# Spreading the gates of a product-key expert layer: bf16 one-hot rows for eight tokens, three gate parts summed in PSUM, splits on VectorE

## The chip, the cores and the metric

One core of one Trainium2 chip runs the whole program in one launch. The metric is the device time of that launch in microseconds, lower is better; the traces give the span from the first to the last instruction of one profiled execution. A core has TensorE (PE, its weight loads shown as PEld), VectorE (DVE), ScalarE (ACT), GpSimd (POOL) and SyncE (SP, which issues the loads here).

## The reference, cut to what matters

256 tokens of width 1024 pass a first block (a delta-net mixer and an expert layer with product keys, PEER) and then a second block of two layers (a token mixer and a routed expert layer each). The change lies in PEER, whose 16384 experts are the pairs of 128 first and 128 second keys:

```python
q = (xt @ w_q).reshape(T, 8, 2, 128)                    # 8 heads, two halves
s = einsum('thpd,hpkd->thpk', q, sub_keys)              # scores against 128 keys each
s1, i1 = top_k(s[:, :, 0], 16); s2, i2 = top_k(s[:, :, 1], 16)
cand_s = s1[..., :, None] + s2[..., None, :]            # 256 candidates
cand_i = i1[..., :, None] * 128 + i2[..., None, :]
top_s, pos = top_k(cand_s, 16); idx = take(cand_i, pos) # 16 experts per head
gate = softmax(top_s)
hid = einsum('td,thkd->thk', xb, u_tab[ib])
coef = gelu(hid) * gb
y = einsum('thk,thkd->td', coef, v_tab[ib])
```

## The kernel before, in words

PEER is computed densely over the experts. `utile(i, tb, eng)` (L917) makes the hidden values of 128 experts (one first key, 128 second keys) for all 256 tokens: `esplit` (L902) loads 128 x 1024 weights (512 KB) into one of three raw places, `split_w` (L39) makes their two parts, the high one on ScalarE (L44) and the low one on the engine that `eng` names (L46), each with three buffers, and `hidden` (L908) multiplies in three passes (L52 to L54), 24 matmuls of 256 columns. ScalarE applies Gelu for the tokens whose gates aren't there yet (L922); for the first `tb` tokens, whose gates are, it goes to `eh` (L925) and VectorE multiplies it into the gates (L926). There are 128 such tiles. The array G[second key, first key, token] holds hidden values, gates and at last their products.

`peer_route` (L928) runs in two stages. In the first, `query(h)` (L945) makes a head's two queries from weights split on GpSimd and `score` their scores; `choose(h)` (L969) takes, on VectorE, the 16 largest of each half (`top16`, L1077), of the 256 sums, and by comparing and reducing (L986 to L994) the two key numbers of each chosen pair, for both halves of the tokens in one go. Behind each head come four hidden tiles, their low parts made on GpSimd, and the query of the head after the next. Softmax gives the gates. Key numbers and gates are then transposed, so that the 128 pairs (head, rank) of a token lie on the partitions (L1024, L1025).

In the second stage G's gates are made by matmul. For four tokens at a time, `onehots` (L1036) compares the key numbers with 0 to 127: L1041 gives the rows of the first key, L1042 those of the second, in f32; L1043 multiplies the first by the high part of the gates, and four ScalarE instructions L1045 by the low part. `spread` (L1048) multiplies the rows of each token, 256 columns (two gate parts side by side, L1052). `gates` (L1054) copies the low sums to SBUF on ScalarE (L1057) and adds the high ones on VectorE, for the experts whose hidden values aren't there (L1059), and for those that are (L1060) with a product by them (L1061). G is written with the tokens innermost, so each token's values are 1 KB apart. Each turn makes one hidden tile besides, with `tb = t0 + 4`.

`peer_experts` (L1086) makes the remaining hidden tiles and multiplies the 128 tiles of values: `vparts` (L1093) splits a value tile on VectorE, and the coefficients into `ech` and `ecl` (L1097, L1098); `vmul` runs 12 matmuls of 512 columns.

The order on each engine is set by the tile framework's scheduler, which takes ready instructions in program order by a model of costs; an engine then works through its queue in that order and waits where an operand isn't there.

Of the kernel before, what the change touches and what calls it, by code (L numbers as in the profile page):

```python
# [33 lines left out]
class Ker:  # L34
# [3 lines left out]
    # ---------------------------------------------------------------- helpers  # L38
    def split_w(self, raw, pool, bufs, tag, eng="gpsimd"):  # L39
        """the two exact parts of raw, in float32r tiles of its shape"""  # L40
        nc = self.nc
        hi = pool.tile(list(raw.shape), F32R, name=tag + "h", bufs=bufs)
        lo = pool.tile(list(raw.shape), F32R, name=tag + "l", bufs=bufs)
        nc.scalar.activation(hi[:], raw, AF.Copy)  # L44
        e = nc.gpsimd if eng == "gpsimd" else nc.vector
        e.tensor_tensor(lo[:], raw, hi[:].bitcast(F32), ALU.subtract)  # L46
        return hi, lo

    def mm3(self, out, L, R, first, last):
        """out += L^T R for operands split in two parts (three passes of float32r)."""  # L50
        mm = self.nc.tensor.matmul
        mm(out, L[0], R[0], start=first, stop=False)  # L52
        mm(out, L[0], R[1], start=False, stop=False)  # L53
        mm(out, L[1], R[0], start=False, stop=last)  # L54

    def consts(self, st):
# [14 lines left out]
        # factors of the rows' norms, sums of squares  # L71
# [3 lines left out]
    def silu_cols(self, cp):  # L75
        """stationary operands of the modulation products"""
# [7 lines left out]
        # stationary operands of the modulation products: 32 columns for each k chunk  # L84
# [9 lines left out]
    # ------------------------------------------------------------ modulations  # L94
    def ada_third(self, key, w, bias, t, wp, wbufs, pp, pt, wk):
        """columns t*2048.. of silu(c) @ w + bias: kept as columns, and as rows in DRAM."""
# [27 lines left out]
        for s in range(ns):  # L124
            # (g, c) order: column 512 g + 128 c
# [3 lines left out]
    def col(self, key, s, chunk):  # L129
        """[128, 8]: the chunk-th 1024 values of the modulation, one column for each k."""  # L130
# [3 lines left out]
    def gate_bcast(self, key, chunk, dst, o=0, w=1024):  # L134
        """dst [128, w] = the chunk-th 1024 values of the modulation from the o-th on, on every partition."""
# [4 lines left out]
    def rstd(self, pool, src, n, mul, add, name):  # L140
        """(src * mul + add) ** -0.5 for src [128, n]"""
# [6 lines left out]
    def rows(self, make, order=((0, 0), (0, 1), (1, 0), (1, 1))):  # L148
        """make(i, j) makes half j of the rows of token tile i of x and returns a place for the squares;
        1/32 of the factors of the rows' norm"""  # L150
# [10 lines left out]
    def norm_T(self, pool, pt, g_cols, sh_cols, dst):  # L161
        """dst(k, ..) <- transpose of x times the row factors, with the column scale and shift"""
# [12 lines left out]
    def mod_parts(self, hh, hl, pool):  # L175
        """dst of norm_T: the two parts of the modulated values, the work shared by three engines"""
# [13 lines left out]
    # ------------------------------------------------------------- delta net  # L190
    def slot(self, n=1):
        """lets the work in the background advance"""
# [10 lines left out]
    def until(self, key):  # L203
        """places are free only after the work of the key"""
# [3 lines left out]
    def delta(self):  # L208
# [12 lines left out]
        # a large negative number where a strictly lower-triangular matrix has zeros  # L221
# [12 lines left out]
        # the projections that come with the norm, and their sums' places  # L234
# [33 lines left out]
    def delta_in(self, cx):  # L268
        """the normed tokens, modulated, a chunk of 128 channels at a time; the first projections follow"""
# [45 lines left out]
        def products(k):  # L315
            """of the vectors' silu and the weights, in four groups of rows"""
# [8 lines left out]
        def columns(k):  # L325
            """shift and scale of the channels, and the two parts of the modulated values"""
# [31 lines left out]
    def delta_gates(self):  # L358
        """beta and the log decays, tokens on partitions: [128, block, (direction, head)]"""
# [28 lines left out]
        # exp of the running sums: eG up to and with a token, eR over those after it, gl over the block  # L388
# [8 lines left out]
        # scalars of the state products: -beta eG (forward), -eG (backward)  # L397
# [4 lines left out]
    def prep(self):  # L402
        """loads and splits the next projection's weights, in two halves"""
# [28 lines left out]
    def conv_silu2(self, ps, ci, ntok):  # L432
        """twice silu of the convolved channels [128, ntok]"""
# [28 lines left out]
    def transposes(self, srcs, pool=None):  # L462
        """one bank with the transposes of up to four blocks"""
# [8 lines left out]
    def l2(self, tp, nb, extra, dst):  # L472
        """dst <- tp / 2 normed over the last axis, times extra ** -0.5"""
# [8 lines left out]
    def gmul(self, out, in0, in1):  # L482
        """out = in0 * in1 on GpSimd"""
        self.nc.gpsimd.tensor_tensor(out, in0, in1, ALU.mult)

    # keys: convolved, normed, and the matrices A of the chunks' systems (I + A) x = b
# [53 lines left out]
    # values and queries  # L540
# [30 lines left out]
    # twice silu of the gate with the norm's weight, tokens on partitions  # L571
# [17 lines left out]
    # in the background  # L589
# [23 lines left out]
    def y_task(self):  # L613
        """the normed, gated output's transposes in two parts"""
# [95 lines left out]
    def delta_out(self):  # L710
        """the output projection, half of its columns and of its rows at a time"""
# [3 lines left out]
        # the output weights take the residual's gate  # L715
# [28 lines left out]
    def add_rows(self, acc, order=((0, 0), (0, 1), (1, 0), (1, 1)), scale=None, gate=None):  # L744
        """x <- x (times the scale of its rows) + acc (times the gate), and the factors of its norm"""
# [12 lines left out]
    def softplus(self, pool, out, x, shape):  # L758
        """max(x, 0) + log1p(exp(-|x|)), the logarithm as 2 atanh(e / (2 + e)) in its series"""
# [18 lines left out]
    def blk_inverse(self, M):  # L778
        """M <- transposes (forward) or the inverses themselves (backward) of I + A, for the 32 strictly
        lower-triangular A in M"""  # L780
        nc, bp, wk, px = self.nc, self.bp, self.wk, self.px
        L = wk.tile([128, 32, 32], F32, name="Lt")   # (r, problem) on partitions: [j][i] = A[i, j]
        T = wk.tile([128, 32, 32], F32, name="Tt")   # [i][c]
        Xc = wk.tile([128, 32, 32], F32, name="Xc", tag="Lt")  # (r, i) on partitions: [problem][c]
# [61 lines left out]
        def s4(q):  # L846
            if q % 2 == 1:  # backward: the inverse itself
# [11 lines left out]
    # ------------------------------------------------------------------ PEER  # L859
    def peer(self):  # L860
        """dense over the experts: hidden values of 128 experts at a time for all tokens, times the
        gates of the chosen ones (zero elsewhere), times the experts' rows"""
# [8 lines left out]
        # the first weights come before the norm  # L871
        self.first = [self.esplit(a["peer_wq"][p], "v") for p in range(2)]
        self.xd = self.dram.tile([128, 2, D], F32, name="xd")
        with ExitStack() as s1:
# [6 lines left out]
            # the residual waits in DRAM; its place takes weights  # L881
# [11 lines left out]
    def rawt(self):  # L893
        """a place for 128 x 1024 raw weights"""
# [7 lines left out]
    def esplit(self, src, eng):  # L902
        """128 x 1024 weights from DRAM in their two parts"""
# [4 lines left out]
    def hidden(self, *Ws):  # L908
        """[128 columns of W, 256 tokens] of the products with the normed tokens, for each W"""
# [7 lines left out]
    def utile(self, i, tb, eng):  # L917
        """hidden values of experts 128 i ..: times the gates for the first tb tokens, whose gates are there"""
# [9 lines left out]
    def peer_route(self, G):  # L928
        """G <- gates, times the hidden values of the first experts, whose number is returned"""
# [4 lines left out]
        idT = [kp.tile([128, 256], F32, name=f"idT{p}") for p in range(2)]  # L934
        gT = kp.tile([128, 256], F32, name="gaT")
# [9 lines left out]
        def query(h):  # L945
# [8 lines left out]
            for p in range(2):  # L954
                ps = P[p] or self.hidden(self.esplit(a["peer_wq"][2 * h + p], "gpsimd"))[0]
# [6 lines left out]
        def score():  # L962
            """of the last query, behind the products that follow it"""
# [5 lines left out]
        def choose(h):  # L969
            sc = wk.tile([128, 2, 2, 128], F32, name="sc", bufs=1)  # L970
            nc.scalar.activation(sc[:], scores[h][:], AF.Copy)
            for i in range(2):
# [3 lines left out]
                for p in range(2):  # L976
                    self.top16(sc[:, i, p, :], v[:, p, :], ix[:, p, :], wk, 128)
                nc.vector.tensor_copy(fx[:], ix[:])
# [4 lines left out]
                self.top16(cand[:].rearrange("p a b -> p (a b)"), top[:, i, h, :], pos[:], wk, 256)  # L983
                ab = wk.tile([128, 2, 16], U32, name="ab")
# [4 lines left out]
                for p in range(2):  # L989
# [4 lines left out]
                    nc.vector.tensor_reduce(sel[p][:, i, h, :], oh[:], mybir.AxisListType.X, ALU.add)  # L994
        ge = []

        def softmax():
            """of the chosen scores"""
# [11 lines left out]
        for h in range(NH):  # L1010
            choose(h)
            if h == NH - 1:
                softmax()
            for _ in range(4):
                self.utile(nu, 0, "gpsimd")
                nu += 1
                score()
            if h + 2 < NH:
                query(h + 2)
        # slots (head, rank) on partitions  # L1020
        for i in range(2):
            tp = pt.tile([128, 4, 128], F32, name="tp")
            for n, (src, dstT) in enumerate(((sel[0][:, i], idT[0]), (sel[1][:, i], idT[1]), (ge[i][:], gT))):
                nc.tensor.transpose(tp[:, n, :], src.rearrange("p h s -> p (h s)"), self.ident)  # L1024
                nc.vector.tensor_copy(dstT[:, i * 128:(i + 1) * 128], tp[:, n, :])  # L1025
        s1.close()
        wk = st.enter_context(tc.tile_pool(reuse_waits="tile", name="p_o", bufs=2))
        ps_g = st.enter_context(tc.tile_pool(reuse_waits="tile", name="p_sg", bufs=2, space=PSUM))
        iota = self.sm("iota").unsqueeze(1).to_broadcast([128, 4, 128])
        # the gates in two exact parts, whose sums come side by side  # L1030
        gh, gl = [kp.tile([128, 256], F32R, name=f"ga{p}") for p in "hl"]
        nc.scalar.activation(gh[:], gT[:], AF.Copy)
        nc.vector.tensor_sub(gl[:], gT[:], gh[:].bitcast(F32))
# [1052 lines left out]
```

## Time and profile before

| | |
|---|---|
| Time, median of 3 runs | 2524.61 us (2518.95 to 2528.83) |
| Profiled execution, span from first to last instruction | 2511.5 us |
| Its time outside the span | not recorded by itself; the median lies 13.1 us above the span |
| Choosing the keys, with 32 hidden tiles | 572 to 763 us of the span |
| Spreading the gates, with 67 hidden tiles | 763 to 1131 us |
| The other hidden tiles, with values | 1131 to 1294.5 us |
| Values alone | 1294.5 to 1566 us |

The stages were cut at the first instructions of the lines that begin them: the copy of the first head's scores (L971), the first one-hot product (L1041), the first coefficients (L1097); and at the end of the last hidden tile's product (L926). How to read it: a share of busy time over the span averages over these stages, so the stages are to be read one by one; and an engine that waits with an instruction already begun counts as busy.

### The profile page before, as it was taken

The numbers are of one execution on the slowest core, as the hardware profiler recorded it, in microseconds if no ns is written. First come the engines' busy times: TensorE is split into PE (matmuls) and PEld (weight loads), VectorE is DVE, ScalarE is ACT, GpSimd is POOL, SyncE is SP. The second block draws the span as 40 slices with busy tenths as digits, with TensorE's granted clock in tenths as the row PEclk, the third lists the DMA queues.
The fourth block names the chain that finished last, engine by engine and source line by source line (L and its number), as shares of the span: only waits on it lengthen the run. The fifth ranks groups of instructions, "written<-read, shape, count | busy, mean of one in ns | idle before, by whom it ended". The sixth has DMA issues, their size and how long they took to land. (4 is left out here: it accounts for less than half of the span.)

```text
span 2511.5 us, 36197 instructions
## 1 busy us (share of the span) xinstructions
PE 2266.3 (90%) x13220; PEld 1619.1 (64%) x13220; DVE 1596.0 (64%) x3069; ACT 950.9 (38%) x2012; POOL 664.9 (26%) x496
## 2 busy tenths in 40 slices
PE   7999999989877777669999999898999989989997
PEld 5445666659877766668988888776444357744432
DVE  4786572458999999994457677877232259733323
ACT  3433434434335555554443333434221133432111
POOL 2443212346644444544420000323000014200000
PEclk9999999989988888989999999999999989989999
DMA  6566564654433232226655555664999636579981
GB/s 255 164 210 191 163 191 154 202 187 157 137 104 109 93 97 92 89 93 195 205 189 190 188 189 181 218 214 150 344 409 386 217 130 216 174 276 407 396 301 60
DMA packets 152607, 497.54 MB, mean 198 GB/s; under 512 B 16960, under 2 KB 18496, under 8 KB 150880
## 3 DMA queue, kind: packets, MB, share of 16 engines
q1 hardware_dynamic: 152416, 495.09, 57.5%
q8 instruction: 108, 1.77, 0.3%
q14 instruction: 83, 0.68, 0.1%
HBM read 492.86 MB, written 2.16 MB: 197 GB/s over the span
## 5 line engine op out<-in xcount | busy, mean ns | idle before, releaser
L52 PE MATMUL hps<-ph,esh 128*128 128x256 f32 x1152 | 349.8, 304 | 25.7 <-ACT G L922 21.5
L54 PE MATMUL hps<-ph,esl 128*128 128x256 f32 x1152 | 347.7, 302 | 8.6 <-POOL esl L46 8.5
L53 PE MATMUL hps<-pl,esh 128*128 128x256 f32 x1152 | 347.1, 301 | 1.0 <-POOL pl L187 1.0
L46 POOL TENSOR_TENSOR esl<-x,esh 128x1024 fp32r<-128x1024 f32 x95 | 244.1, 2572 | 256.1 <-ACT esh L44 237.1
L1898 PE MATMUL pg<-wgu,xe 128*64 128x512 f32 x1024 | 276.3, 601 | 0.0
L52 PEld LDWEIGHTS hps<-ph,esh 128*128 128x128 f32 x1152 | 243.9, 212 | 29.1 <-ACT G L922 23.0
L44 ACT ACTIVATE esh<-x 128x1024 fp32r<-128x1024 f32 x170 | 179.4, 1055 | 207.0 <-PE y L54 120.6
L54 PEld LDWEIGHTS hps<-ph,esl 128*128 128x128 f32 x1152 | 242.4, 210 | 10.8 <-POOL esl L46 10.8
L53 PEld LDWEIGHTS hps<-pl,esh 128*128 128x128 f32 x1152 | 243.1, 211 | 2.3 <-POOL pl L187 1.2
L52 PE MATMUL y<-esh,ech 128*128 128x512 f32 x512 | 201.7, 394 | 1.3 <-ACT esh L44 1.3
L54 PE MATMUL y<-esh,ecl 128*128 128x512 f32 x512 | 202.0, 394 | 0.0
L53 PE MATMUL y<-esl,ech 128*128 128x512 f32 x512 | 201.9, 394 | 0.0
L1898 PEld LDWEIGHTS pg<-wgu,xe 128*64 128x64 f32 x1024 | 79.0, 137 | 131.8 <-issue 123.9
L1041 DVE TENSOR_TENSOR om<-small,idT 128x512 f32<-128x512 f32 x64 | 155.2, 2425 | 1.7 <-ACT o L1045 1.7
L46 POOL TENSOR_TENSOR esl<-raw,esh 128x1024 fp32r<-128x1024 f32 x47 | 120.4, 2561 | 107.8 <-ACT esh L44 100.9
L106 PE MATMUL adaps<-adaw,cst 128*32 128x512 f32 x512 | 139.7, 608 | 9.7 <-DMA adaw<-in_ada_w_dram 5.9
L46 DVE TENSOR_TENSOR esl<-x,esh 128x1024 fp32r<-128x1024 f32 x75 | 91.9, 1226 | 86.9 <-ACT esh L44 86.9
L1052 PE MATMUL gp<-o,o 128*128 128x256 f32 x256 | 50.2, 323 | 98.5 <-ACT esh L44 77.6
L44 ACT ACTIVATE esh<-raw 128x1024 fp32r<-128x1024 f32 x92 | 97.1, 1056 | 99.9 <-PE y L54 68.9
L46 DVE TENSOR_TENSOR wrsl<-wr,wrsh 128x512 fp32r<-128x512 f32 x135 | 104.5, 788 | 34.9 <-ACT wrsh L44 33.9
L1930 PE MATMUL pw<-wdn,hTs 128*64 128x512 f32 x512 | 124.1, 597 | 0.0
L1045 ACT ACTIVATE o<-om,gal 128x128 fp32r<-128x128 f32 x256 | 81.8, 390 | 108.3 <-DVE om L1041 105.7
(610 smaller groups left out, 4925.2 us busy)
## 6 DMA issues: line engine op xcount, KB each, us to landing
wgu<-in_w_gu_dram SPq DMA_DIRECT2D x256, 512.0 KB, 10.2
wdn<-in_w_d_dram SPq DMA_DIRECT2D x128, 512.0 KB, 7.4
adaw<-in_w_ada_dram SPq DMA_DIRECT2D x96, 512.0 KB, 4.3
x<-in_peer_u_dram SPq DMA_DIRECT2D x81, 512.0 KB, 3.7
x<-in_peer_v_dram SPq DMA_DIRECT2D x75, 512.0 KB, 4.3
raw<-in_peer_u_dram SPq DMA_DIRECT2D x47, 512.0 KB, 3.9
raw<-in_peer_v_dram SPq DMA_DIRECT2D x43, 512.0 KB, 4.3
dw<-in_dn_w_dram SPq DMA_DIRECT2D x64, 256.0 KB, 4.5
```

Of the source, the lines that this page charges most:

```text
L44: nc.scalar.activation(hi[:], raw, AF.Copy)
L46: e.tensor_tensor(lo[:], raw, hi[:].bitcast(F32), ALU.subtract)
L52: mm(out, L[0], R[0], start=first, stop=False)
L53: mm(out, L[0], R[1], start=False, stop=False)
L54: mm(out, L[1], R[0], start=False, stop=last)
L106: nc.tensor.matmul(ps[g * 32:(g + 1) * 32, :], self.cst[:, which, k, :], wt[:, v * 512:(v + 1) * 512], start=k == 0, stop=k == KC - 1)
L1041: nc.vector.tensor_tensor(m[:], iota, b(idT[0]), ALU.is_equal)
L1045: nc.scalar.activation(o1[:, t, 1, :], m[:, t, :], AF.Copy, scale=gl[:, t0 + t:t0 + t + 1].bitcast(F32))
L1052: nc.tensor.matmul(gp[:, t], o2[:, t, :], o1[:, t], start=True, stop=True)
L1898: mm(gu[p][j * 64:j * 64 + 64, :], xe[p // 2][:, k, s0:s0 + 64], wt[2 * p + j, 0, k // 2][:, k % 2, :], start=k == 0, stop=k == KC - 1)
L1930: mm(ps[j * 64:j * 64 + 64, :], hT[p][:, f, j * 64:j * 64 + 64], wt[2 * p + j, 1, f][:, n * 512:(n + 1) * 512], start=f == 0, stop=f == 1)
```

## The change

- Key numbers and one-hot rows are bf16. `onehots` works on eight tokens, with the token innermost: five VectorE products of 128 x 1024 bf16 elements, each over a stored array of the numbers 0 to 127 (`keys`) and a row of eight values that is read again for each key.
- The gates are split in three bf16 parts; `spread` runs three matmuls of 128 columns for each token, which add in PSUM, and reads both operands at a step of eight elements. There are four PSUM places of one bank in place of two of two banks.
- `gates` copies the sums for the experts without hidden values on ScalarE, and multiplies them into G on VectorE for those with.
- `choose` gives way three times for each half of the tokens, and a hidden tile follows each time: 48 in this stage in place of 32.
- The low parts of queries and hidden tiles are made on VectorE, in all stages.

The comments and docstrings of the whole file are left out as well. The core of the diff:

```diff
-        idT = [kp.tile([128, 256], F32, name=f"idT{p}") for p in range(2)]
-        gT = kp.tile([128, 256], F32, name="gaT")
+        idT = [kp.tile([128, 256], BF16, name=f"idT{p}") for p in range(2)]
+        gT = [kp.tile([128, 256], BF16, name=f"ga{p}") for p in "hml"]
...
-                ps = P[p] or self.hidden(self.esplit(a["peer_wq"][2 * h + p], "gpsimd"))[0]
+                ps = P[p] or self.hidden(self.esplit(a["peer_wq"][2 * h + p], "vector"))[0]
...
                     self.top16(sc[:, i, p, :], v[:, p, :], ix[:, p, :], wk, 128)
+                yield
...
                 self.top16(cand[:].rearrange("p a b -> p (a b)"), top[:, i, h, :], pos[:], wk, 256)
+                yield
...
                     nc.vector.tensor_reduce(sel[p][:, i, h, :], oh[:], mybir.AxisListType.X, ALU.add)
+                yield
...
-            choose(h)
+            for _ in choose(h):
+                self.utile(nu, 0, "vector")
+                nu += 1
+                score()
             if h == NH - 1:
                 softmax()
-            for _ in range(4):
-                self.utile(nu, 0, "gpsimd")
-                nu += 1
-                score()
...
+            rest = tp[:, 2, :]
+            for p in range(3):
+                nc.scalar.activation(gT[p][:, t], rest, AF.Copy)
+                if p < 2:
+                    r = wk.tile([128, 128], F32, name="gr")
+                    nc.vector.tensor_tensor(r[:], rest, gT[p][:, t], ALU.subtract)
+                    rest = r[:]
...
+        NT = 8
+        keys = wk.tile([128, 128, NT], BF16, name="keys", bufs=1)
+        nc.vector.tensor_copy(keys[:], self.sm("iota").unsqueeze(2).to_broadcast([128, 128, NT]))
...
         def onehots(t0):
-            b = lambda t: t[:, t0:t0 + 4].unsqueeze(2).to_broadcast([128, 4, 128])
-            m = wk.tile([128, 4, 128], F32, name="om", bufs=1)
-            o1 = wk.tile([128, 4, 2, 128], F32R, name="o1", bufs=2)
-            o2 = wk.tile([128, 4, 128], F32R, name="o2", bufs=2)
-            nc.vector.tensor_tensor(m[:], iota, b(idT[0]), ALU.is_equal)
-            nc.vector.tensor_tensor(o2[:], iota, b(idT[1]), ALU.is_equal)
-            nc.vector.tensor_tensor(o1[:, :, 0, :], m[:], b(gh[:].bitcast(F32)), ALU.mult)
+
+            b = lambda t: t[:, t0:t0 + NT].unsqueeze(1).to_broadcast([128, 128, NT])
+            o1 = [wk.tile([128, 128, NT], BF16, name=f"o1{p}") for p in "hml"]
+            o2 = wk.tile([128, 128, NT], BF16, name="o2")
+            nc.vector.tensor_tensor(o2[:], keys[:], b(idT[1]), ALU.is_equal)
+            m = o1[2]
+            nc.vector.tensor_tensor(m[:], keys[:], b(idT[0]), ALU.is_equal)
+            for p in range(3):
+                nc.vector.tensor_tensor(o1[p][:], m[:], b(gT[p]), ALU.mult)
+            ohs[t0] = o1, o2
+
+        def spread(t0):
+
+            o1, o2 = ohs[t0 // NT * NT]
+            gp = gps[t0] = ps_g.tile([128, 4, 128], F32, name="gp")
             for t in range(4):
-                nc.scalar.activation(o1[:, t, 1, :], m[:, t, :], AF.Copy, scale=gl[:, t0 + t:t0 + t + 1].bitcast(F32))
-            ohs[t0] = o1, o2
-
-        def spread(t0):
-            o1, o2 = ohs.pop(t0)
-            gp = gps[t0] = ps_g.tile([128, 4, 2, 128], F32, name="gp")
-            for t in range(4):
-                nc.tensor.matmul(gp[:, t], o2[:, t, :], o1[:, t], start=True, stop=True)
+                c = t0 % NT + t
+                for p in range(3):
+                    nc.tensor.matmul(gp[:, t, :], o2[:, :, c], o1[p][:, :, c], start=p == 0, stop=p == 2)
 
         def gates(t0):
             gp = gps.pop(t0)
-            lo = wk.tile([128, 4, 128], F32, name="glo", bufs=1)
-            nc.scalar.activation(lo[:], gp[:, :, 1, :], AF.Copy)
             g = G[:, :, t0:t0 + 4].rearrange("p e t -> p t e")
-            nc.vector.tensor_tensor(g[:, :, nu:128], gp[:, :, 0, nu:128], lo[:, :, nu:128], ALU.add)
-            nc.vector.tensor_tensor(lo[:, :, 0:nu], gp[:, :, 0, 0:nu], lo[:, :, 0:nu], ALU.add)
-            nc.vector.tensor_tensor(g[:, :, 0:nu], g[:, :, 0:nu], lo[:, :, 0:nu], ALU.mult)
+            nc.scalar.activation(g[:, :, nu:128], gp[:, :, nu:128], AF.Copy)
+            nc.vector.tensor_tensor(g[:, :, 0:nu], g[:, :, 0:nu], gp[:, :, 0:nu], ALU.mult)
...
         for t0 in range(0, 256, 4):
             spread(t0)
-            if t0 + 4 < 256:
-                onehots(t0 + 4)
+            if t0 % NT == 0 and t0 + NT < 256:
+                onehots(t0 + NT)
             gates(t0)
             if nu < 124:
-                self.utile(nu, t0 + 4, "gpsimd")
+                self.utile(nu, t0 + 4, "vector")
                 nu += 1
```

## Rows read from the trace of the kernel before

**Rows 1.** The page, busy us (share of the span) and instructions of each engine, with the span.
```profile
span 2511.5 us, 36197 instructions
...
PE 2266.3 (90%) x13220; PEld 1619.1 (64%) x13220; DVE 1596.0 (64%) x3069; ACT 950.9 (38%) x2012; POOL 664.9 (26%) x496
```

**Rows 2.** Busy time by stage: us, then PE, PEld, DVE, ACT, POOL, clock, DMA, GB/s.
```profile
core 0: us, PE busy (x) PEld busy (x) DVE busy (x) ACT busy (x) POOL busy (x), PEclk, DMA share, GB/s
572.00:763.00 191.00, 156.14 (x1159) 152.28 (x1158) 183.46 (x574) 69.38 (x106) 111.02 (x47) 0.88 0.41 136
763.00:1131.00 368.00, 269.55 (x1856) 259.43 (x1855) 363.90 (x450) 204.65 (x518) 178.81 (x66) 0.89 0.29 94
1131.00:1294.50 163.50, 162.19 (x1032) 146.99 (x1032) 70.20 (x128) 69.42 (x87) 67.53 (x28) 1.00 0.62 199
1294.50:1566.00 271.50, 271.50 (x1170) 219.84 (x1169) 189.96 (x304) 103.47 (x99) 0.00 (x0) 1.00 0.58 189
```

**Rows 3.** Groups of VectorE, 763 to 1131: count, busy us, mean ns, idle before.
```profile
L1041 DVE TENSOR_TENSOR om<-small,idT 128x512 f32<-128x512 f32 x64 | 155.2, 2425 | 1.7 <-ACT o L1045 1.7
L1042 DVE TENSOR_TENSOR o<-small,idT 128x512 fp32r<-128x512 f32 x64 | 54.1, 847 | 0.0
```

**Rows 4.** Timeline of one turn: start us, us, engine, line, op, tiles.
```profile
903.29 2.72 POOL L46 TENSOR_TENSOR esl<-x,esh 128x1024 fp32r<-128x1024 f32 x1 [2.88 <-ACT esh L44]
...
903.74 2.82 DVE L1041 TENSOR_TENSOR om<-small,idT 128x512 f32<-128x512 f32 x1
...
906.47 0.68 DVE L1042 TENSOR_TENSOR o<-small,idT 128x512 fp32r<-128x512 f32 x1
...
909.36 2.80 DVE L1041 TENSOR_TENSOR om<-small,idT 128x512 f32<-128x512 f32 x1
```

**Rows 5.** Waits, 763 to 1131: us in total, times, longest.
```profile
ACT o L1045 <- DVE om L1041: 105.7, 53, 2.1
...
PE gp L1052 <- ACT esh L44: 77.6, 51, 2.3
```

**Rows 6.** Groups, 572 to 763, and two lines' least/median/greatest ns.
```profile
L993 DVE TENSOR_TENSOR oh<-oh,tf 128x256 f32<-128x256 f32 x32 | 29.9, 933 | 0.4
L991 DVE TENSOR_TENSOR oh<-small,abf 128x256 f32<-128x256 f32 x32 | 27.3, 852 | 0.4
L986 DVE TENSOR_SCALAR ab<-pos 128x16 uint32<-128x16 uint32 x16 | 15.8, 986 | 0.4
...
L988 DVE CAST abf<-ab 128x32 f32<-128x32 uint32 x16 | 13.1, 821 | 0.2
...
L922 ACT ACTIVATE G<-hps 128x256 f32<-128x256 f32 x32 | 12.1, 378 | 0.0
...
L993 DVE TENSOR_TENSOR oh<-oh,tf x32: 400/408/2633, 582.1 to 752.9; 128x256 f32<-128x256 f32 x32
...
L988 DVE CAST abf<-ab x16: 164/174/2264, 581.2 to 749.0; 128x32 f32<-128x32 uint32 x16
```

**Rows 7.** Timeline of TensorE, at full and at half clock.
```profile
591.75 0.28 PE L54 MATMUL hps<-ph,esl 128*128 128x256 f32 x1
...
592.11 0.28 PE L54 MATMUL hps<-ph,esl 128*128 128x256 f32 x1
...
592.60 0.60 PE L967 MATMUL ss<-kt,qTs 128*128 128x128 f32 x4
592.96 0.36 PE L52 MATMUL hps<-ph,esh 128*128 128x256 f32 x1
...
909.98 0.42 PE L52 MATMUL hps<-ph,esh 128*128 128x256 f32 x1
...
910.62 0.41 PE L52 MATMUL hps<-ph,esh 128*128 128x256 f32 x1
```

**Rows 8.** Timeline of VectorE in the gates' loop and after it.
```profile
879.83 0.22 DVE L926 TENSOR_TENSOR G<-eh,G 128x76 f32<-128x76 f32 x1
...
880.88 0.65 DVE L1061 TENSOR_TENSOR G<-G,glo 128x216 f32<-128x216 f32 x1
...
1105.20 1.03 DVE L1061 TENSOR_TENSOR G<-G,glo 128x372 f32<-128x372 f32 x1
...
1135.49 1.22 DVE L46 TENSOR_TENSOR esl<-raw,esh 128x1024 fp32r<-128x1024 f32 x1
1136.62 0.42 DVE L926 TENSOR_TENSOR G<-eh,G 128x256 f32<-128x256 f32 x1
```

More of the change, by code (lines that the diff above doesn't have):

```diff
@@ L1022, in peer_route @@
             tp = pt.tile([128, 4, 128], F32, name="tp")
-            for n, (src, dstT) in enumerate(((sel[0][:, i], idT[0]), (sel[1][:, i], idT[1]), (ge[i][:], gT))):
+            for n, src in enumerate((sel[0][:, i], sel[1][:, i], ge[i][:])):
                 nc.tensor.transpose(tp[:, n, :], src.rearrange("p h s -> p (h s)"), self.ident)
-                nc.vector.tensor_copy(dstT[:, i * 128:(i + 1) * 128], tp[:, n, :])
+            t = slice(i * 128, (i + 1) * 128)
+            for p in range(2):
+                nc.vector.tensor_copy(idT[p][:, t], tp[:, p, :])
@@ L1026, in peer_route @@
+            rest = tp[:, 2, :]
[5 more added lines that the diff above has]
+                    rest = r[:]
         s1.close()
         wk = st.enter_context(tc.tile_pool(reuse_waits="tile", name="p_o", bufs=2))
-        ps_g = st.enter_context(tc.tile_pool(reuse_waits="tile", name="p_sg", bufs=2, space=PSUM))
@@ L1029, in peer_route @@
[L1029 to L1033, printed above, removed]
-        gps, ohs = {}, {}
-        def onehots(t0):
-            b = lambda t: t[:, t0:t0 + 4].unsqueeze(2).to_broadcast([128, 4, 128])
-            m = wk.tile([128, 4, 128], F32, name="om", bufs=1)
-            o1 = wk.tile([128, 4, 2, 128], F32R, name="o1", bufs=2)
-            o2 = wk.tile([128, 4, 128], F32R, name="o2", bufs=2)
-            nc.vector.tensor_tensor(m[:], iota, b(idT[0]), ALU.is_equal)
-            nc.vector.tensor_tensor(o2[:], iota, b(idT[1]), ALU.is_equal)
-            nc.vector.tensor_tensor(o1[:, :, 0, :], m[:], b(gh[:].bitcast(F32)), ALU.mult)
-            for t in range(4):
-                nc.scalar.activation(o1[:, t, 1, :], m[:, t, :], AF.Copy, scale=gl[:, t0 + t:t0 + t + 1].bitcast(F32))
+        ps_g = st.enter_context(tc.tile_pool(reuse_waits="tile", name="p_sg", bufs=4, space=PSUM))
@@ new lines, in peer_route @@
+        NT = 8
+        keys = wk.tile([128, 128, NT], BF16, name="keys", bufs=1)
+        nc.vector.tensor_copy(keys[:], self.sm("iota").unsqueeze(2).to_broadcast([128, 128, NT]))
+        ohs, gps = {}, {}
+        def onehots(t0):
+            b = lambda t: t[:, t0:t0 + NT].unsqueeze(1).to_broadcast([128, 128, NT])
[6 more added lines that the diff above has]
+                nc.vector.tensor_tensor(o1[p][:], m[:], b(gT[p]), ALU.mult)
@@ L1062, in peer_route @@
+            nc.vector.tensor_tensor(g[:, :, 0:nu], g[:, :, 0:nu], gp[:, :, 0:nu], ALU.mult)
         onehots(0)
         for _ in range(3):
-            self.utile(nu, 0, "gpsimd")
+            self.utile(nu, 0, "vector")
             nu += 1
@@ L1106, in peer_experts @@
             if nu < NT:
-                self.utile(nu, 256, "gpsimd")
+                self.utile(nu, 256, "vector")
                 nu += 1
```

## The prediction

> **What bounds the kernel now.** I read the page's busy line first, then busy time by stage, then the stages' own groups, timelines and waits. The page has TensorE busy for 90% of the span [rows 1], but that is an average. By stage [rows 2], the change touches three of the four stages of the first block's experts. In the stage where keys are chosen (572 to 763) VectorE is busy for 183.5 of 191 us and TensorE for 156; in the stage where the gates are spread (763 to 1131) VectorE for 363.9 of 368 and TensorE for 269.6 at a granted clock of 0.89; from 1131 on TensorE is busy for all but 1.3 us. So VectorE bounds the first two stages, TensorE the last two.
>
> VectorE's time there is not all work. The reader should look at one turn of the gates' loop [rows 4]: GpSimd's split runs from 903.29 to 906.01, and the product L1041, started at 903.74, ends only at 906.56. The same form takes 0.68 us as L1042 right behind it. Over the stage L1041 averages 2425 ns and L1042 847 [rows 3]: against 0.68 that is 64 x 1.74 + 64 x 0.17 = 122 us in which VectorE stands with an instruction open while GpSimd works. The turn is 909.36 - 903.74 = 5.62 us. TensorE in turn stands idle behind the one-hot rows: its matmul L1052 waited 51 times, 77.6 us in all [rows 5]. The wait is put down to ScalarE's L44, which stands right behind L1045, and L1045 waited 53 times for L1041, 105.7 us. In the choosing stage the same happens to L993, L991, L986 and L988 [rows 6]: against least times of 0.40 us (256 elements) and 0.16 us (16 or 32), the excess is 32 x 0.53 + 32 x 0.45 + 16 x 0.82 + 16 x 0.66 = 55 us.
>
> **Prices.** TensorE: three matmuls of a hidden tile start 0.36 us apart (591.75 to 592.11), so a tile of 24 costs 2.88 us, and twice about 0.21 each at half clock (909.98 to 910.62); four matmuls of 128 columns take 592.96 - 592.60 = 0.36, 0.09 each [rows 7]. VectorE: a split of 1024 elements lasts 1.22 us and the next instruction starts 1.13 after it; I take 0.09 off every duration below for that overlap. L1061, with the gates' strided reads and writes, lasts 0.65 at 216 elements and 1.03 at 372; L926 0.22 at 76 and 0.42 at 256 [rows 8].
>
> **Part 1: choosing in pieces, splits on VectorE.** Each head yields six times instead of running four tiles, so 48 hidden tiles fall into this stage in place of 32, and 14 queries as before. GpSimd's work goes, and its 55 us of blocking: VectorE keeps 183.5 - 55 = 128 us and gains 62 splits x 1.13 = 70, together 198. TensorE needs 62 x 2.88 = 179 plus 64 x 0.09 = 6 of scores, 185. With both so near the stage's length I add about 3.5% of mutual waiting: 205 us, against 191, **+14**. Bounds: 198 (+7) and 225 (TensorE as busy as now, 82%: +34). In VectorE's queue, behind a split that waits for ScalarE's L44, stand the pieces of the choice; L44 itself waits for the 512 KB load. The loads need 62 x 0.524 MB in 205 us = 159 GB/s, where the stage from 1131 moves 199 [rows 2], so they stay covered; SyncE's queue issues them in the same order as now. If not covered, 62 tiles at 199 GB/s are 163 us, still below.
>
> **Part 2: the gates' loop.** It still has 64 turns of four tokens, one hidden tile in each. Every second turn makes one-hot rows of eight tokens: five products of 1024 bf16 elements. No row shows a product of two bf16 operands. Bounds: 1024 elements of f32, 1.13 us [rows 8], and the same bytes, which is 512 f32 elements, 0.68 - 0.09 = 0.59 [rows 4]. I take 0.59, since a row of as many bytes is the nearer one; that is 1.48 us a turn (2.83 at the other end). [...]
>
> The sum of both gate parts is left to PSUM, so L1060 and one of the two strided products go to nothing and to ScalarE. One strided product stays; the first tiles now number 51 to 114, on average 330 elements, which L1061's rows put at 0.84 us. L926 averages 130 elements: 0.19. The split 1.13. VectorE: 1.48 + 0.84 + 0.19 + 1.13 = **3.64 us a turn**. ScalarE loses four L1045 and L1057 and gains a copy of about 180 elements; it is busy for 205 of 368 now [rows 2], so no bound.
>
> TensorE gets 12 matmuls of 128 columns a turn for four of 256. At 0.09 each that is 1.08, so 2.88 + 1.08 = **3.96 us a turn**. Below, half of it (half the bytes): 3.42, and VectorE's 3.64 would set the turn. Above: both operands are read at a step of eight elements, which no row of TensorE shows. On VectorE the strided L1061 costs (1.03 - 0.65)/156 = 2.4 ns an element against 0.59/512 = 1.15 for a dense one [rows 4, 8], a factor 2.1; 0.19 x 12 = 2.3 gives 5.15 a turn. [...]
>
> With two engines near 3.8 I take 4.2 a turn (6% of waiting; the stage from 1131 to 1294, with VectorE less loaded, has 1%). The stage: 10 us of head (three tiles, the transposes, the split of the gates in three parts, which runs beside the tiles) + 64 x 4.2 = 279, against 368: **-89**. Uncovered, the head's chain of copies would add some 4 us.
>
> **Part 3: the last stage.** 48 + 3 + 64 = 115 tiles are done when it begins, in place of 99, so 16 tiles leave it: 16 x 2.88 = **-46**, at full price since TensorE is busy throughout [rows 2]. The splits that move here cost VectorE 1.13 per pair of tile and value tile, and it is busy for 70 of 163.5 us: hidden. Uncovered, 13 x 1.13 = 15 us.
>
> **Sum.** 14 - 89 - 46 = -121 on the span of 2511.5 [rows 1], so 2390.5. The median of the runs, 2524.6, is 13.1 above the span; I carry this over: **2404 us**. The change in the rest (delta net, second block) is nothing: no instruction of it is touched.
>
> **Rivals.**
> - *The bf16 products cost by element, or the strided reads cost double.* VectorE then needs 4.99 a turn, or TensorE 5.15. Each gives about 5.2, so 10 + 333 = 343: -25 + 14 - 46 = -57, **2468 us**. For it: nothing in the profile shows either form. Chance 0.25; this is also the case in which the bf16 part does not do what it says.
> - *No mutual waiting.* The turn falls to 3.64 (cheap matmuls), the choice to 198: 7 - 125 - 46 = -164, **2361**; at 3.96 it is 2381. For it: the stage from 1131 runs at 99%. Chance 0.09.
> - *Slower: VectorE's queue becomes a chain.* If the split of the next tile is queued behind L926, which waits for the tile on TensorE, a turn is 2.88 (tile) + 0.38 (the Gelu, L922 [rows 6]) + 0.33 (L926) + 1.48 + 0.84 + 1.13 = 7.0 us; 10 + 448 = 458: +90 + 14 - 46 = +58, **2583**. It decides from a turn of 6.1 us on (10 + 64 x 6.1 = 400 = 368 + 46 - 14). Against it: at 1135.49 a split stands ahead of L926 in VectorE's queue [rows 8], so the order lets a split pass a product that waits. Chance 0.06.
> - *No change within 0.5%* (12.6 us, about what a measurement tells from none): a turn near 6 us, 0.03.
>
> **Numbers.** The forecast, 2404, has a chance of 0.57, with its own range of 2382 to 2435 (turns of 3.9 to 4.6, choice 198 to 215). The range for 8 in 10 goes from 2362 to 2475, by the second and the first rival. Faster 0.91, same 0.03, slower 0.06.
>
> **What would show it.** Right: GpSimd idle from the first choice to the end of the value tiles; no VectorE product over 1.3 us there; the 1024-element bf16 products near 0.68 us; turns of 4.2 us; the clock in the loop near 1.0; 13 hidden tiles after the loop. Wrong: bf16 products of 1.2 us, matmuls of the spread 0.18 apart, TensorE waiting for VectorE's splits, or a choosing stage beyond 225 us.

## The result and the profile after

The changed kernel takes **2546.5 us** (median of 5 runs, 2541.8 to 2556.2) against 2525.9 for the kernel before, measured beside it (median of 5, 2519.0 to 2533.4): a ratio of 1.0084, 95% interval 1.0057 to 1.0111. The forecast was 2404, range 2362 to 2475. It is slower by 0.8%, where 121 us of gain were expected.

First the page of the changed kernel, with the busy time of each engine; it answers to [rows 1].

```profile
span 2546.1 us, 36618 instructions
...
PE 2441.5 (96%) x13732; PEld 1732.8 (68%) x13732; DVE 1496.2 (59%) x3037; ACT 875.5 (34%) x1761; POOL 303.5 (12%) x354
```

VectorE has 100 us less to do and GpSimd 361 less, as the change intends, but TensorE is busy 175 us longer, with only 512 instructions more. The stages say where. These are busy times by stage, with the same cuts as [rows 2] (the third row takes the two stages from 1131 to 1566 together, the fourth is all that follows).

```profile
core 0: us, PE busy (x) PEld busy (x) DVE busy (x) ACT busy (x) POOL busy (x), PEclk, DMA share, GB/s
572.00:776.00 204.00, 201.58 (x1642) 197.97 (x1642) 191.88 (x642) 99.00 (x151) 0.00 (x0) 1.00 0.51 175
776.00:1209.00 433.00, 432.85 (x2307) 369.00 (x2306) 243.13 (x354) 122.23 (x258) 0.00 (x0) 0.82 0.23 80
1209.00:1600.00 391.00, 391.00 (x1841) 324.81 (x1841) 268.37 (x426) 152.82 (x155) 0.00 (x0) 1.00 0.57 193
1600.00:2546.00 946.00, 876.71 (x4597) 512.99 (x4595) 457.86 (x901) 274.79 (x561) 127.36 (x133) 0.96 0.70 259
```

Choosing lasts 204 us (forecast 205), the stage of the values 391 (163.5 + 271.5 - 46 = 389), the rest 946 as before (2511.5 - 1566 = 945.5). The stage of the gates lasts **433** where 279 was forecast: 154 us, the whole miss on the span. In it VectorE is busy for 243 of 433 us and TensorE is counted busy for all of it, at a granted clock of 0.82. The bound has gone over from VectorE to TensorE.

The groups of that stage (count, busy us, mean ns, idle before and by whom it ended) and its waits (us in total, times, longest) answer to [rows 3] and [rows 5]:

```profile
L52 PE MATMUL hps<-ph,esh 128*128 128x256 f32 x513 | 191.1, 373 | 0.0
L1067 PE MATMUL gp<-o1h,o 128*128 128x128 bf16 x256 | 107.0, 418 | 0.2 <-DVE o1h L1057 0.2
L1067 PEld LDWEIGHTS <-o 128*128 128x128 bf16 x768 | 106.6, 147 | 57.3 <-DVE o1h L1057 0.4
L1073 DVE TENSOR_TENSOR G<-G,gp 128x204 f32<-128x204 f32 (+31 forms) x64 | 57.6, 901 | 39.9 <-ACT G L1072 39.8
L46 DVE TENSOR_TENSOR esl<-x,esh 128x1024 fp32r<-128x1024 f32 x44 | 53.6, 1218 | 11.0 <-ACT esh L44 11.0
L1053 DVE TENSOR_TENSOR o<-keys,idT 128x1024 bf16<-128x1024 bf16 x32 | 22.2, 692 | 113.4 <-PE gp L1067 113.3
L1057 DVE TENSOR_TENSOR o1l<-o1l,gal 128x1024 bf16<-128x1024 bf16 x32 | 21.9, 684 | 0.0
```
```profile
DVE o L1053 <- PE gp L1067: 113.3, 29, 5.8
ACT G L1072 <- PE gp L1067: 101.4, 64, 3.0
```

The blocked VectorE product of 2425 ns is gone and the bf16 products last 0.69 us, as forecast. VectorE and ScalarE now wait for the spread's matmul, L1067. Its turn on TensorE (start us, duration), for [rows 4] and [rows 7]:

```profile
905.18 0.43 PE L1067 MATMUL gp<-o1h,o 128*128 128x128 bf16 x1
905.43 0.41 PE L1067 MATMUL gp<-o1m,o 128*128 128x128 bf16 x1
905.67 0.41 PE L1067 MATMUL gp<-o1l,o 128*128 128x128 bf16 x1
...
907.77 0.41 PE L1067 MATMUL gp<-o1l,o 128*128 128x128 bf16 x1
907.82 0.57 PE L52 MATMUL hps<-ph,esh 128*128 128x256 f32 x1
908.20 0.41 PE L53 MATMUL hps<-pl,esh 128*128 128x256 f32 x1
908.41 0.41 PE L54 MATMUL hps<-ph,esl 128*128 128x256 f32 x1
...
911.40 0.29 PE L53 MATMUL hps<-pl,esh 128*128 128x256 f32 x1
911.52 0.28 PE L54 MATMUL hps<-ph,esl 128*128 128x256 f32 x1
...
912.36 0.43 PE L1067 MATMUL gp<-o1h,o 128*128 128x128 bf16 x1
```

The reader is to see two things. The twelve matmuls start (907.77 - 905.18)/11 = 0.235 us apart, not 0.09. And the hidden tile behind them takes 912.36 - 907.82 = 4.54 us instead of 2.88: its matmuls stand 0.21 apart up to about 911.2 and 0.12 after. The windows of the two pieces show the granted clock:

```profile
905.18:907.82 2.64, 2.64 (x14) 1.71 (x13) 0.00 (x0) 1.39 (x3) 0.00 (x0) 1.00 0.00 0
907.82:912.36 4.54, 4.54 (x27) 4.48 (x25) 4.14 (x7) 0.58 (x1) 0.00 (x0) 0.62 0.00 0
```

During the strided matmuls VectorE does nothing and the granted clock is 1.00; in the tile behind it is 0.62 on the mean, 0.52 up to 911.20 and 0.91 after, and TensorE is counted busy for all of both windows. These two sizes give the stage: 768 matmuls at 0.235 are 180 us where 768 at 0.09 were 69, **+111**; the other 433 - 180 = 253 us hold the matmuls of 64 tiles (513 in each of the three passes, eight a tile), which at 0.12 would need 185, **+68** for the half clock. Less 9 for three tiles (3 x 2.88) that the forecast counted in this stage and that lie outside its cuts, and less the 16 us of mutual waiting that were allowed for (279 - 10 - 64 x 3.96) and that a TensorE without gaps doesn't have: 111 + 68 - 9 - 16 = 154, which is what is missing.

In the choosing stage the groups answer to [rows 6] (count, busy us, mean ns):

```profile
L995 DVE TENSOR_TENSOR oh<-small,abf 128x256 f32<-128x256 f32 x32 | 13.3, 416 | 0.3
L997 DVE TENSOR_TENSOR oh<-oh,tf 128x256 f32<-128x256 f32 x32 | 13.3, 415 | 0.2
...
L990 DVE TENSOR_SCALAR ab<-pos 128x16 uint32<-128x16 uint32 x16 | 2.7, 170 | 0.2
```

With GpSimd out of the way all three stand at the least times that they had before: 0.42 where the means were 0.85 and 0.93, 0.17 where it was 0.99.

### The profile page after: what moved, and what is told of

Its sections match the earlier page's. It is cut to its first block, busy times and chain, and to the rows that moved or that the text cites. A ratio compares the mean times of both kernels' runs of the same rounds, so it can differ in the third digit from the quotient of the medians.

```text
span 2546.1 us, 36618 instructions
## 1 busy us (share of the span) xinstructions
PE 2441.5 (96%) x13732; PEld 1732.8 (68%) x13732; DVE 1496.2 (59%) x3037; ACT 875.5 (34%) x1761; POOL 303.5 (12%) x354
## 5 line engine op out<-in xcount | busy, mean ns | idle before, releaser
L52 PE MATMUL hps<-ph,esh 128*128 128x256 f32 x1152 | 374.9, 325 | 4.2 <-ACT esh L44 3.5
L54 PE MATMUL hps<-ph,esl 128*128 128x256 f32 x1152 | 359.2, 312 | 1.8 <-DVE esl L46 1.4
L53 PE MATMUL hps<-pl,esh 128*128 128x256 f32 x1152 | 359.0, 312 | 1.0 <-POOL pl L187 1.0
L53 PEld LDWEIGHTS hps<-pl,esh 128*128 128x128 f32 x1152 | 258.4, 224 | 3.0 <-POOL pl L187 1.3
L54 PEld LDWEIGHTS hps<-ph,esl 128*128 128x128 f32 x1152 | 254.1, 221 | 4.8 <-DVE esl L46 4.7
L46 DVE TENSOR_TENSOR esl<-x,esh 128x1024 fp32r<-128x1024 f32 x170 | 207.4, 1220 | 67.4 <-ACT esh L44 67.4
L1067 PEld LDWEIGHTS <-o 128*128 128x128 bf16 x768 | 106.6, 147 | 57.3 <-DVE o1h L1057 0.4
L46 DVE TENSOR_TENSOR esl<-raw,esh 128x1024 fp32r<-128x1024 f32 x92 | 112.3, 1221 | 34.3 <-ACT esh L44 34.3
L44 ACT ACTIVATE wrsh<-wr 128x512 fp32r<-128x512 f32 x137 | 84.8, 628 | 89.2 <-PE pj L54 57.8
L54 PEld LDWEIGHTS y<-esh,ecl 128*128 128x128 f32 x512 | 96.4, 188 | 22.5
```

Of the source, the lines that this page charges most:

```text
L1067: nc.tensor.matmul(gp[:, t, :], o2[:, :, c], o1[p][:, :, c], start=p == 0, stop=p == 2)
```

## The experiments

The theory after the result: the reads of the spread's operands at a step of eight bf16 elements make its matmul slow. A matmul has two operands: the stationary one, which LDWEIGHTS loads (here `o`, the second keys' rows), and the moving one, which MATMUL reads (here `o1`, the gates' rows). The rivals: it is the count of matmuls or PSUM that costs, whatever is read; or it is only one of the two operands. All ratios are to the kernel before on the same chip.

**Which operand.** Three kernels read 128 elements in a row in place of every eighth: of both operands, of the moving one, of the stationary one. The gates that they spread are other numbers.

```diff
-                    nc.tensor.matmul(gp[:, t, :], o2[:, :, c], o1[p][:, :, c], start=p == 0, stop=p == 2)
+                    d = lambda a: a[:].rearrange("p k t -> p (k t)")[:, c * 128:(c + 1) * 128]
+                    nc.tensor.matmul(gp[:, t, :], d(o2), d(o1[p]), start=p == 0, stop=p == 2)       # both
+                    nc.tensor.matmul(gp[:, t, :], o2[:, :, c], d(o1[p]), start=p == 0, stop=p == 2) # moving
+                    nc.tensor.matmul(gp[:, t, :], d(o2), o1[p][:, :, c], start=p == 0, stop=p == 2) # stationary
```

> The changed kernel with both operands of the spread's matmuls read densely (128 neighbouring elements of the same arrays in place of every eighth); the gates it spreads are other numbers, all instructions and sizes are the same. Theory A (the step of eight elements is what costs): the spread's matmuls start 0.12 us apart or less in place of 0.235, the hidden tile behind them runs at full clock, a turn of the gates' loop takes 3.96 to 4.4 us in place of 6.6 on average, and the time falls by about 64 x 2.4 = 150 us, to 2375 to 2415. Rival B (three matmuls with a weight load each in place of one are the cost, whatever the step): matmuls still about 0.23 apart, time within 0.5% of the changed kernel, about 2546. Rival C (VectorE's queue is the cost): turn still near 6.6, TensorE idle where it is busy now.

> Only the moving operand (gate rows) is read densely, the stationary one at a step of eight; the gates spread are other numbers. If the moving operand's step is what costs: like the run with both dense, about 2395. If the weight load's step is: like the changed kernel, 2546. If each has its share: between them.

> Only the stationary operand (key rows) is read densely, the moving one at a step of eight; the gates spread are other numbers. The counterpart of the run before: about 2546 if the moving operand's step is what costs, about 2395 if the weight load's is.

Measured: both dense 2352.5 us (median of 4), ratio 0.933 (0.928 to 0.938); moving dense 2344.5 (one run, 0.931); stationary dense 2488.8 (one run, 0.988). The first two lie below what was expected of them (2375 to 2415, and 2395): their matmuls cost less than the 0.12 that was allowed, and the turn falls to VectorE's, 3.65 us with both dense. TensorE's timelines of the moving-dense and then of the stationary-dense kernel (start us, duration):

```profile
902.03 0.23 PE L1068 MATMUL gp<-o1l,o 128*128 128x128 bf16 x1
902.09 0.22 PE L1068 MATMUL gp<-o1h,o 128*128 128x128 bf16 x1
902.15 0.23 PE L1068 MATMUL gp<-o1m,o 128*128 128x128 bf16 x1
```
```profile
902.15 0.41 PE L1068 MATMUL gp<-o1m,o 128*128 128x128 bf16 x1
902.38 0.41 PE L1068 MATMUL gp<-o1l,o 128*128 128x128 bf16 x1
...
904.47 0.48 PE L52 MATMUL hps<-ph,esh 128*128 128x256 f32 x1
904.78 0.28 PE L53 MATMUL hps<-pl,esh 128*128 128x256 f32 x1
...
907.55 0.39 PE L1068 MATMUL gp<-o1h,o 128*128 128x128 bf16 x1
```

The matmuls stand 0.06 us apart in the one and 0.23 in the other. So it is the moving operand's step, not the count of matmuls or PSUM. The stationary operand's step is paid in the weight loads, 147 ns with it against 98 in the kernel with both dense, and they run beside the matmuls:

```profile
L1068 PEld LDWEIGHTS <-o 128*128 128x128 bf16 x768 | 43.1, 98 | 3.1 <-DVE o1h L1057 0.4
```

The busy times of the gates' stage with both dense, with the moving operand dense and with the stationary one dense show the rest:

```profile
781.00:1020.00 239.00, 236.27 (x2328) 231.68 (x2327) 236.40 (x353) 116.85 (x259) 0.00 (x0) 1.00 0.43 143
```
```profile
761.00:1004.00 243.00, 242.11 (x2330) 238.51 (x2329) 238.47 (x353) 116.71 (x259) 0.00 (x0) 1.00 0.43 141
```
```profile
767.00:1150.00 383.00, 382.85 (x2306) 301.60 (x2306) 242.85 (x354) 121.91 (x258) 0.00 (x0) 0.93 0.27 90
```

With only the moving operand strided the clock is 0.93 in place of 0.82, and many tiles run at full clock, as the one from 904.47 to 907.55. A turn is then 907.55 - 901.95 = 5.60 us, 12 x 0.225 + 2.88 = 5.58: this is the matmul's price without the clock's. Of the 50 us between 433 and 383, 768 x 0.01 = 8 are the matmul's (0.225 against 0.235); the rest is the clock, which falls further with both steps, though the numbers multiplied are others here too, so that the step's own part in it is not told apart.

**The size of the step.** Four tokens at once (8 bytes), and two (4 bytes).

```diff
-        NT = 8
+        NT = 4      # and 2, with two such groups a turn
```

> The changed kernel with four tokens at once in place of eight: the step of both operands is four elements (8 bytes), five VectorE products of 512 bf16 elements each turn, about 0.35 us apart, so 1.75 in place of 1.48 a turn. Theory A with a cost that hangs on the step: the matmuls come closer together than 0.235 us; if a step of 8 bytes costs nothing, 0.09 to 0.12, a turn of about 4.3 us and a time of 2385 to 2425. If any step costs as much as this one: 0.235 and 2546 or a little more.

> The changed kernel with two tokens at once: both operands are read at a step of two elements (4 bytes); VectorE makes ten products of 256 bf16 elements a turn, about 0.2 us each, 2.0 in place of 1.48. If the matmul's price goes with the moving operand's step (0.235 at eight, 0.118 at four, 0.057 dense): 0.06 to 0.065 apart, VectorE sets a turn of about 4.2, time about 2380. If there is a fixed price for any step above one: 0.11 or so.

Measured: four tokens 2388.3 us (median of 4), ratio 0.947 (0.942 to 0.952); two tokens 2394.1 (one run, 0.947). The first lines of a spread with four tokens:

```profile
901.67 0.30 PE L1067 MATMUL gp<-o1m,o 128*128 128x128 bf16 x1
901.79 0.30 PE L1067 MATMUL gp<-o1l,o 128*128 128x128 bf16 x1
901.90 0.30 PE L1067 MATMUL gp<-o1h,o 128*128 128x128 bf16 x1
```

They start 0.117 apart; with two tokens 0.06, as dense. So the step costs next to nothing at 4 bytes, twice the dense time at 8 and four times at 16. With four tokens TensorE still sets the stage (275.9 of 276 us, clock 1.00); with two it is VectorE (busy for 244.1 of 247 us, 780 to 1027), whose products of 256 elements last 301 ns, ten a turn. Each takes about 0.20 us of its time, an estimate: the groups of that window add up to 321.3 us, 77 more than VectorE is busy, an overlap of 0.10 for each of 773 instructions. A quarter of the 0.60 between two products of 1024 (in the kernel with pairs, below) would be 0.15.

**Less of the strided work.** Only the first of the three gate parts is multiplied; the products on VectorE stay.

```diff
-                    nc.tensor.matmul(gp[:, t, :], o2[:, :, c], o1[p][:, :, c], start=p == 0, stop=p == 2)
+                    if p == 0:
+                        nc.tensor.matmul(gp[:, t, :], o2[:, :, c], o1[p][:, :, c], start=True, stop=True)
```

> Leaves out two of the three parts of the gates in the spread (one strided matmul a token in place of three; the products on VectorE stay). Theory (a matmul at the step of 16 bytes costs 0.235 us, and many of them in a row pull the granted clock of the hidden tile behind them down): 4 x 0.235 = 0.94 a turn, tile at full clock 2.88, so a turn of about 3.85 and a loop of about 255, clock near 1.0, whole kernel 2355 to 2380. Rival (the clock falls with any strided matmul, however few): the tiles behind still run at half clock in part, loop above 290, clock below 0.9, whole kernel above 2395.

Measured: 2363.4 us (one run, 0.936). The stage:

```profile
782.00:1024.00 242.00, 240.79 (x1730) 220.57 (x1731) 229.27 (x342) 115.14 (x249) 0.00 (x0) 0.99 0.41 131
```

Its strided matmuls last as long as before (mean 416 ns), the stage has a clock of 0.99 and the tiles behind run at 0.12 a matmul. So a strided matmul has its price at full clock too, and the fall of the clock comes on top of it with all three parts. What the chip goes by in that stays open.

**The rest of the change alone.** The kernel before with the choice in pieces and all splits on VectorE, but with the old f32 one-hot rows.

```diff
-                ps = P[p] or self.hidden(self.esplit(a["peer_wq"][2 * h + p], "gpsimd"))[0]
+                ps = P[p] or self.hidden(self.esplit(a["peer_wq"][2 * h + p], "vector"))[0]
...
-            choose(h)
+            for _ in choose(h):
+                self.utile(nu, 0, "vector")
+                nu += 1
+                score()
```

> The kernel before with the choice in pieces and all splits on VectorE, but with its f32 one-hot rows of four tokens, ScalarE's low part and the two-part sum. Theory (the new rows' reads are what costs, the rest of the change gains as forecast): choosing stage about 204 us, values stage about 390, loop by VectorE at 3 x 0.61 + 0.36 + 0.44 + 0.84 + 0.19 + 1.13 = 4.8 us a turn, 10 + 64 x 4.9 = 324; together 76 us less than before, about 2443, and 100 below the changed kernel. Rival (the splits on VectorE or the pieces cost the time): near the changed kernel, 2520 to 2550.

Measured: 2420.2 us (median of 4), ratio 0.956 (0.951 to 0.962). The product that averaged 2425 ns [rows 3], L1043 here, from 780 to 1050:

```profile
L1043 DVE TENSOR_TENSOR om<-small,idT 128x512 f32<-128x512 f32 x59 | 39.4, 669 | 0.0
```

GpSimd, whose split was what held VectorE, is busy for 0.00 us here. This part gains 107 us by itself, more than the 76 expected: a turn of the loop takes 4.6 us where 4.9 was allowed. The new rows with their strided reads take away all of it and some 20 more.

**Keeping eight tokens without the step.** Two kernels put the gates on the stationary side, whose step costs little (147 against 98 ns a load, beside the matmuls), and make the moving rows plain: in the first by one compare that reads each key number again for 128 neighbours (`iob` holds the numbers 0 to 127 in bf16), in the second by a tensor_scalar for each token.

```diff
-            o1 = [wk.tile([128, 128, NT], BF16, name=f"o1{p}") for p in "hml"]
-            o2 = wk.tile([128, 128, NT], BF16, name="o2")
+            o2 = [wk.tile([128, 128, NT], BF16, name=f"o2{p}") for p in "hml"]
+            o1 = wk.tile([128, NT, 128], BF16, name="o1")
+            nc.vector.tensor_tensor(o1[:], iob[:].unsqueeze(1).to_broadcast([128, NT, 128]),
+                                    idT[0][:, t0:t0 + NT].unsqueeze(2).to_broadcast([128, NT, 128]), ALU.is_equal)
...
+                    nc.tensor.matmul(gp[:, t, :], o2[p][:, :, c], o1[:, c, :], start=p == 0, stop=p == 2)
```

> The changed kernel with the gate parts on the other operand: the three products of key rows and gates are the stationary operands, still at a step of eight, and the plain one-hot rows of the first key are the moving one, written token by token and read densely. One of VectorE's five products then has its eight values along the rows and is expected at the price of 1024 f32 elements, 1.13 us, in place of 0.6. Theory (only the moving operand's step costs): matmuls 0.06 apart as with the moving operand dense, clock full in the loop; VectorE 1.77 + 0.84 + 0.19 + 1.13 = 3.93 us a turn sets the loop, 0.29 above the run with the moving operand dense, so 2344 + 64 x 0.29 = 2363, 2350 to 2375. Rival (the weight load's step costs as soon as three different weights follow each other): matmuls near 0.15, 2400 or more.

> As the run before, but the moving rows are made by eight VectorE compares of 128 elements with one key number for each partition. If one of them starts 0.08 us after the other, as the shortest VectorE instructions do, 0.64 in place of 1.13 for eight tokens: a turn of 3.7 us, about 2350. If each costs 0.15: 1.2, as the run before, about 2365.

Measured: 2372.6 us (median of 4), ratio 0.940 (0.935 to 0.945), and 2385.7, 0.944 (0.940 to 0.949). The compare of the first lasts 1219 ns, where the four other bf16 products have 0.69; the 128-element tensor_scalars of the second last 273 ns on the mean, and 256 of them keep VectorE busy for 54.6 us, so eight take 1.7 us, more than either price that was expected, and the time lies above both. (The shortest VectorE instructions of the changed kernel's choosing stage, MATCH_VALUE_LOADs, have means of 73 to 87 ns.) Both ways cost VectorE more than the compare that they replace, and VectorE sets the stage (busy for 246.1 of 247 us in the first, 243.6 in the second).

The last one stores the eight tokens as four pairs, so that the step is 4 bytes and the products keep 1024 elements.

```diff
-            b = lambda t: t[:, t0:t0 + NT].unsqueeze(1).to_broadcast([128, 128, NT])
-            o1 = [wk.tile([128, 128, NT], BF16, name=f"o1{p}") for p in "hml"]
+            b = lambda t: t[:, t0:t0 + NT].rearrange("p (g u) -> p g u", u=2).unsqueeze(2).to_broadcast([128, 4, 128, 2])
+            kk = keys[:].unsqueeze(1).to_broadcast([128, 4, 128, 2])
+            o1 = [wk.tile([128, 4, 128, 2], BF16, name=f"o1{p}") for p in "hml"]
...
-                    nc.tensor.matmul(gp[:, t, :], o2[:, :, c], o1[p][:, :, c], start=p == 0, stop=p == 2)
+                    nc.tensor.matmul(gp[:, t, :], o2[:, c // 2, :, c % 2], o1[p][:, c // 2, :, c % 2], start=p == 0, stop=p == 2)
```

> The rows of eight tokens stand as four pairs: key by key the two tokens of a pair are neighbours, so that the matmul reads at a step of two elements (4 bytes), and the five products of a turn are still of 1024 bf16 elements. Theory (the step of the spread's reads sets the price): matmuls 0.06 us apart as with two tokens at once, products still 0.69, loop of the gates 243 to 250 us at a granted clock near 1.0, whole kernel 2344 to 2362, ratio to before about 0.93. Rival (what counts is that eight tokens share a tile, or the products lose their price by pairs of two elements): matmuls above 0.1 apart or products of 1.2 us, loop above 275, whole kernel above 2380.

Measured: **2353.8 us** (median of 4), ratio 0.932 (0.929 to 0.935): 172 us below the kernel before on the same chip, 193 below the changed one's 2546.5. Against the 107 us of the other parts, the new rows now gain some 65 more. Two of its spread's matmuls, a product, and the stage of the gates:

```profile
903.18 0.22 PE L1068 MATMUL gp<-o1m,o 128*128 128x128 bf16 x1
903.24 0.22 PE L1068 MATMUL gp<-o1l,o 128*128 128x128 bf16 x1
```
```profile
L1056 DVE TENSOR_TENSOR o1l<-keys,idT 128x1024 bf16<-128x1024 bf16 x32 | 21.8, 680 | 0.0
```
```profile
782.00:1024.00 242.00, 240.00 (x2345) 235.15 (x2344) 239.55 (x360) 118.22 (x258) 0.00 (x0) 1.00 0.43 143
```

Both engines are now counted busy for all but some 2 us of 242, at a granted clock of 1.00.

## Why the prediction failed, point by point

- **The step that failed is the price of the spread's matmuls**, "At 0.09 each that is 1.08" a turn. It came from a dense f32 matmul, though the prediction itself noted that no row of TensorE shows a read at a step of eight. Measured 0.235, so 2.82 a turn: 111 of the 154 us missing. The upper bound was too low as well: 0.19, from VectorE's strided L1061, whose factor of 2.1 is that of an 8-byte step on TensorE (0.117 against 0.057 in the kernel with both dense), not that of a 16-byte step (4.1).
- **The half clock was priced nowhere.** The forecast was a clock near 1.0 in the loop; it is 0.82, and 68 us of the miss are hidden tiles at half clock. Of the kernels with bf16 rows, the dense, the paired and the four-token ones have a clock of 1.00, and only those with all three parts read at 16 bytes by the moving operand fall to 0.82 and 0.93; the kernel with one part in place of three, at the same 16 bytes, has 0.99, and what the chip goes by between the two stays open. Such reads are not all that lowers it: the kernel before, without them, has 0.89 in its stage [rows 2].
- The first rival named the mechanism, strided reads at double cost (2468, chance 0.25), and its size was short by both terms. With 0.235 in place of 0.19 and no clock loss it would give 10 + 64 x 5.70 = 375 for the stage, 7 above the 368 before, and with the +14 and -46 of the other stages 25 us below the kernel before. The clock then carries it over to the slower side. (The kernel with only the moving operand strided, 30 below the one before, has 0.225 and still a clock of 0.93.) The slower rival, VectorE's queue as a chain, did not come: VectorE has 190 us of slack in the stage. Its boundary held, a turn of 6.1 us: from the first matmul of the first spread (781.4) to that of the last (1205.5) are 63 turns of 6.7. A slower kernel had a chance of 0.06, and came by another way.
- **Right:** VectorE's turn. With 0.09 off each for the overlap, two and a half products are 1.49 (forecast 1.48), L1073 0.81 (0.84), L926 0.20 (0.19), the split 1.13: 3.63 against 3.64. A product of 1024 bf16 elements lasts 0.69 us where the split of 1024 f32 elements lasts 1.22, and the bf16 compare that reads each key number again for 128 neighbours lasts 1.22 too.
- Right: GpSimd's blocking and its end, and the 16 tiles taken out of the last stage. The choosing stage's 204 us (forecast 205) are in part luck: TensorE, not VectorE, is the engine that fills it (201.6 of 204 against 191.9), since it holds the matmuls of 65 tiles and queries where 62 were counted.
- The 13.1 us that were added outside the span were not there: every run whose span is on record lies some 1.8 us above it. With that the profiled execution of the kernel before would have taken 2513.3 us, less than any of its five timed runs, so the spans differ by 34.6 us and the medians by 20.6.
- The inner range doesn't follow from its own terms: turns of 3.9 to 4.6 and a choice of 198 to 215 give 2377 to 2439, not 2382 to 2435.
- The sum with the right prices: the paired kernel, which changes only how the rows are stored, is 172 us below the kernel before, more than the 121 forecast. From the first matmul of its first spread (781.8) to that of its last (1012.1) are 63 turns of 3.66 us, what VectorE's work asks for, without the mutual waiting that the forecast allowed.

## What to carry to other kernels

Before a layout is chosen that is cheap to write for VectorE, price how TensorE reads it: here a moving operand of bf16 wanted its elements at most 4 bytes apart (0.06 us a matmul, against 0.117 at 8 bytes and 0.235 at 16), while the stationary one could be strided at little cost (147 against 98 ns a load), since its loads ran beside the matmuls. Where the trace has no row for a form, the forecast should lean to the row that shares its access pattern (the strided one), not its size. Eight tokens can be kept in one VectorE product as pairs: the products keep their price (0.68 us) and the matmuls theirs (0.06).

## What was unexpected of the hardware

- A 128-column bf16 matmul follows its predecessor by 0.057 us with a dense moving operand, 0.06 at a step of 4 bytes, 0.117 at 8 and 0.225 to 0.235 at 16. A stationary operand at a step of 16 bytes lengthens its load from 98 to 147 ns.
- TensorE, counted busy for all but 2.8 us of the stage or less, was granted 0.82 of its clock over the stage with both operands strided, 0.93 with the moving one alone, and 1.00 with the stationary one alone or none. The fall shows in the f32 matmuls behind the strided ones (0.21 us apart against 0.12), not in the window of the strided ones themselves (1.00).
- A small VectorE instruction is dear for its size: products of 256 bf16 elements last 301 ns and take about 0.20 us of its time each (the estimate above), tensor_scalars of 128 elements last 273 ns and take 0.21, against 680 ns and starts 0.60 us apart for products of 1024.
